# Low halves of 112 weight slots: adding transfers from GpSimd in place of VectorE subtractions, with the negated high half written by ScalarE

## The chip, the core and the metric

The kernel runs on one core of one Trainium2 chip. The core has a matrix engine (TensorE, PE in the profile; its weight loads are the row PEld), VectorE (DVE), ScalarE (ACT), GpSimd (POOL), and SyncE (SP), which here only issues transfers. Sixteen DMA engines move data between the device's memory and the core's on-chip memory. Each compute engine takes its instructions in a fixed order, and an instruction whose input is not ready holds up everything behind it on that engine. The metric is the device time of one execution in microseconds.

## What is computed

Two layers of a decoder on 1024 tokens of width 1024, all in float32. Layer 0 is sliding-window attention (16 query heads, 2 key/value heads, window 128, a learned sink per head, partial rotary), layer 1 a gated linear recurrence (HGRN2, 8 heads). Both have one input projection that also makes a SiLU gate, and an output projection, and each sits between two RMS norms.

```python
def attention_mixer(h, positions, w_in, b_in, sinks, w_out, b_out):
    proj = h @ w_in + b_in
    q, k, v, z = jnp.split(proj, [...], axis=-1)
    ...
    o = sliding_window_gqa(q, k, v, sinks)
    return (o * jax.nn.silu(z)) @ w_out + b_out

def hgrn2_mixer(h, lower_bound, w_in, gnorm_w, w_out):
    proj = h @ w_in
    q, f, i, z = jnp.split(proj, [...], axis=-1)
    ...
    o = chunked_gated_recurrence(q, k, v, log_f)
    o = o * lax.rsqrt(jnp.mean(o * o, axis=-1, keepdims=True) + NORM_EPS) * gnorm_w
    return (o * jax.nn.silu(z)) @ w_out

    for layer in range(DEPTH):
        h = rmsnorm(x, pre_norm_w[layer])
        y = attention_mixer(...) if layer % 2 == 0 else hgrn2_mixer(...)
        x = x + rmsnorm(y, post_norm_w[layer])
```

The four products with weights (`h @ w_in`, `... @ w_out`, twice) are what the change concerns.

## The kernel before

**Split products.** Every product with weights runs as three matmuls of a shorter float type (float32r). Each operand x is split exactly into a high half hi, which is x rounded to that type, and a low half lo = x - hi. `product` (L186 to L189) adds hi*hi, hi*lo and lo*hi into one accumulator. So every weight has to exist twice in on-chip memory, as `whi` and `wlo`.

**The stream of weight slots.** All weights lie in the device's memory as 132 slots of 128 x 512 numbers (256 KB), in the order of use. `fetch` (L131) loads a slot into one of four raw buffers `wraw` by a transfer that SP issues; slot i+4 goes into the buffer of slot i when that is split. `advance` (L137) splits the next slots as far as there are places: ten pairs of `whi` and `wlo` (and two of their own for slots 10 and 11, the keys' weights). For slots 0 to 19 GpSimd makes the high half (L152). From slot 20 on, which is 112 slots, ScalarE makes it by a copy that rounds (L154). The low half is then made by a subtraction, raw - hi (L155), on VectorE, except for slots 2 and 3, which GpSimd subtracts.

**How slots are used and freed.** `used` (L158) counts reads; a slot has eight, and behind the eighth its place is given to the next slot. The projections come in two kinds:

- feature-major (`proj_feat`, L191): a unit makes 128 columns for 512 tokens; two slots hold these columns for all 1024 rows, each is read four times, and a second unit for the other 512 tokens reads them again. Slots 0 to 35 (layer 0's input), 60 to 75 and 84 to 99 (queries and forget gates of layer 1) are of this kind.
- token-major (`proj_nat`, L200): a unit makes 512 columns for 128 tokens; eight slots make a chunk, and each of the chunk's eight units reads all eight slots once, in their order. Slots 36 to 43 and 44 to 51 (layer 0's output, two chunks), 52 to 59 and 76 to 83 (values of layer 1), 100 to 107 and 108 to 115 (its gate), 116 to 123 and 124 to 131 (its output).

A unit has eight steps, one for each 128 rows, and a step is the three matmuls of `product`. In the token-major kind the order is act_hi x whi, act_hi x wlo, act_lo x whi.

**What sets the order.** A planner orders the instructions of each engine by a simulated timeline and priorities; the weight splits have a raised priority (`hp`, L118), so that they go before the work that they make room for. Attention units, projection units and the recurrence's heads are emitted in an order written out by hand (`at`, L577 and following, for layer 0; `plan`, L855 and following, for layer 1).

**Other lines that are named below.** L87 is a helper that passes VectorE instructions on in program order, used at the start. L179 and L180 split activations into halves (ScalarE, VectorE) on their way out of a transpose. In layer 0's last part L615 and L616 take the output projection in, L639 and L640 scale it and add x (VectorE, and GpSimd for one half of L640), L224, L214 and L216 form the reciprocal root mean square `rstd` (ScalarE, GpSimd), L229 normalises (`hn`), and L236 transposes. L473 forms the attention's gates (`th`), L553 masks the probabilities (`pT`). L839 transposes the recurrence's gated output, L846 to L848 gate it, L885, L886 and L888 take the last output projection in.

Of the kernel before, what the change touches and what calls it, by code (L numbers as in the profile page):

```python
# [2 lines left out]
"""Two-layer hybrid decoder trunk (sliding-window attention, then HGRN2) on one core.  # L3

Dense products run as three single-pass float32r products of exactly split operands
(x = hi + lo with 12 significant bits each; hi*hi + hi*lo + lo*hi), which keeps float32's
accuracy.  The other products are plain float32.
"""
# [4 lines left out]
F32 = mybir.dt.float32  # L13
# [19 lines left out]
# rotary frequencies 500000 ** (-j / 8) in float32  # L33
# [17 lines left out]
# columns of the packed constant array  # L51
C_ID, C_INV, C_BIN, C_PRE, C_LB, C_GN, C_SINK = 0, 128, 129, 147, 163, 179, 180
C_N = 196
# columns of the mask array: two for the attention, seven tree levels, causal within blocks of 32
M_L, M_D, M_N = 2 * P, 2 * P + 7 * 64, 3 * P + 7 * 64
# the cheap form of the recurrence's chunks needs every forget gate above this bound
LB_MIN = 2.0 ** -6
LGT_MAX = 4.125  # so that 1 / (1 + exp(LGT_MAX)) > LB_MIN
# [9 lines left out]
# rows of a head in the scores' products: rotated dimensions at 0..8 and 32..40  # L68
# [10 lines left out]
class InOrder:  # L79
    """an engine whose instructions keep the program's order while .on is set"""  # L80
# [9 lines left out]
def emit(tc, I, out):  # L90
# [4 lines left out]
    with top:  # L95
# [22 lines left out]
        def hp():  # L118
            """evictions and weight splits go before the work they make room for"""
            return tc.high_priority(offset=HP)  # L120

        # ---------------- weights: stream of [128, 512] slots, split into hi and lo
# [14 lines left out]
        def advance(end=NS):  # L137
            """fetch and split the next slots, as far as places are free (in program order)"""
            while W["split"] < end:
                i = W["split"]  # L140
                fetch(i + NR)
                if i in (W_K, W_K + 1):
                    W["place"][i] = W["keys"][i - W_K]
                elif W["free"]:
                    W["place"][i] = W["free"].pop(0)
                else:
                    return
                raw, (hi, lo) = wraw[i % NR], W["place"][i]
                with hp():
                    on_pool = i in (2, 3)  # L150
                    if i < 20:
                        nc.gpsimd.tensor_scalar(hi, raw, 1.0, 1.0, op0=ALU.mult, op1=ALU.mult)  # L152
                    else:
                        nc.scalar.activation(hi, raw, AF.Copy)  # L154
                    W["split_ins"][i] = (nc.gpsimd if on_pool else v).tensor_tensor(lo, raw, hi.bitcast(F32), op=ALU.subtract)  # L155
                W["split"] += 1

        def used(i):  # L158
            """one of the eight reads of slot i has been emitted"""
            W["left"][i] = W["left"].get(i, 8) - 1  # L160
            if W["left"][i] == 0:
                if i not in (W_K, W_K + 1):
                    W["free"].append(W["place"][i])
                advance()

        def weight(first, k, c0, c1):
            """hi and lo of columns c0..c1 of the k-th 128 rows of a chunk"""
            hi, lo = W["place"][first + k]
            return hi[:, c0:c1], lo[:, c0:c1]

        # ---------------- activations (feature-major, hi and lo), [k][half]
        act = {(k, h): (actp.tile([P, 512], F32R, name=f"acth{k}_{h}"), actp.tile([P, 512], F32R, name=f"actl{k}_{h}"))
               for k in range(NK) for h in range(2)}
        # at first x, then the first heads' attention, then layer 1's first value columns
# [16 lines left out]
        def proj_feat(first, half):  # L191
            """feature-major [128 columns, 512 tokens]; two slots hold the 128 columns of all k"""
            ps = mm()
            for k in range(NK):
                c = (k % 4) * P
                product(ps, k, weight(first, k // 4, c, c + P), act[k, half])
                used(first + k // 4)
            return ps

        def proj_nat(first, t, c0=0, c1=512, tag="mm"):  # L200
            """token-major [128 tokens, columns c0 to c1 of 512]"""
            ps = mm((P, c1 - c0), tag)
            c = slice((t % 4) * P, (t % 4 + 1) * P)
            for k in range(NK):
                hi, lo = act[k, t // 4]
                product(ps, k, (hi[:, c], lo[:, c]), weight(first, k, c0, c1))
                if c1 == 512:
                    used(first + k)
            return ps

        def rstd_of(pool, ms, width, eps=EPS):
            """(ms + eps) ** -0.5 on [128, width]"""
            m = pool.tile([P, width], F32, tag="ms", bufs=4, name="ms")
            nc.gpsimd.tensor_scalar(m, ms, eps, 1.0, op0=ALU.add, op1=ALU.mult)  # L214
            r = pool.tile([P, width], F32, tag="rstd", bufs=4, name="rstd")
            W["rstd"] = nc.gpsimd.tensor_tensor(r, m, nhalf[:, :width], op=ALU.pow)  # L216
            return r

        def row_rstd(pool, xt, junk=None):
            """of the rows of xt (SBUF [128, 1024])"""  # L220
            if junk is None:
                junk = pool.tile([P, D], F32, tag="jkx", name="jkx")
            ms = pool.tile([P, 1], F32, tag="ss", bufs=4, name="ss")
            nc.scalar.activation(junk, xt, AF.Square, scale=D ** -0.5, accum_out=ms)  # L224
            return rstd_of(pool, ms, 1)

        def norm_rows(pool, xt, hn, r=None):
            """rows of xt over their root mean square"""
# [12 lines left out]
        # =====================================================================  # L241
        # layer 0
# [6 lines left out]
        def halves(t):  # L249
            """columns by which the t-th rows of x are taken; the first half's last rows go in two steps"""  # L250
            return [slice(0, 512), slice(512, D)] if t == 3 else [slice(0, D)]
# [7 lines left out]
        def lower_bounds(sp):  # L259
            """layer 1's lower bounds: softmax over the two rows of logits"""  # L260
# [11 lines left out]
        def rope_tables(sp, cosT, sinT, cosK, tK):  # L272
            """rotary tables; the steps to the angles on [(j, chunk), 64], in turns, and what follows them"""
# [6 lines left out]
            def neg_frac(x):  # L280
                """x = round(x) - x, in two steps"""
# [42 lines left out]
        # =====================================================================  # L324
        # layer 0
        def layer0():
            """attention mixer up to its gated output; leaves x + mixer in x1d and its norm in act"""
# [8 lines left out]
            # of 128 keys from 64 before each block, and the last 64 keys twice  # L336
# [126 lines left out]
            with pool("att", "right") as ap:  # L463
                def z_unit(p, half):
                    ps = proj_feat(20 + 2 * (p ^ 4), half)
                    with hp():
# [4 lines left out]
                        # the last heads' last gates come before their attention, the others after  # L471
# [9 lines left out]
                def values_twice(g, b):  # L481
                    """for the blocks b and b + 1, twice: the former block's earlier 64 keys and the block's later ones"""
# [9 lines left out]
                def attn(g, b):  # L492
# [6 lines left out]
                    for par in range(2):  # L499
                        o = par * 64  # L500
                        # scores of the 128 keys a query may see (their slots: see host_arrays), and 8 x the sink
# [7 lines left out]
                        for hp in range(2):  # L509
# [8 lines left out]
                            # the slots of the block's later half and of the former block's earlier half  # L518
# [21 lines left out]
                        # what lies outside of the 128 keys from 64 before the block, hi and lo below each other  # L540
# [35 lines left out]
                # how many of them to emit behind each attention unit  # L576
# [70 lines left out]
        # =====================================================================  # L647
        # layer 1
        def mixer1(fast, vo, rp):
# [34 lines left out]
            def scores_tree(X, F, Y):  # L684
                """scores[s, t] of all chunks for any gates: products over a binary tree, none above 1.
                Turns X and Y into the queries from the chunk's start and the keys to its end."""
# [43 lines left out]
            def scores_block(h, Q, F, K):  # L730
                """as scores_tree, for gates above LB_MIN: inside blocks of 32 the decay from s to t is a
                quotient of running products from the block's middle, each within LB_MIN ** -16."""
                sc = scs[h % 2]
                # running products of blocks of 16: U up to and with a token, V behind it
# [134 lines left out]
        def output1(fp, last_half):  # L869
# [5 lines left out]
            def unit(c, t):  # L875
                y = fp.tile([P, 512], F32, tag=f"y{c}", bufs=(8, 2)[c], name="y")
                jk = fp.tile([P, 512], F32, tag="jk", name="jk")
                # the last unit in two steps, so that less is left to do at the end
# [41 lines left out]
        # which way the recurrence goes: its lower bounds are 1 / (1 + exp(difference of the logits))  # L920
# [33 lines left out]
def host_arrays(x, positions, pre_norm_w, post_norm_w, attn_w_in, attn_b_in, attn_sinks, attn_w_out, attn_b_out,  # L954
                rec_w_in, rec_lb_logits, rec_gnorm_w, rec_w_out):
    def slots(w):
        """[1024, n * 512] -> [n * 8, 128, 512]"""
# [3 lines left out]
    def slots_feat(w):  # L961
        """[1024, n * 128] -> [n * 2, 128, 4 * 128]: 128 columns of four 128-row blocks to a slot"""
# [27 lines left out]
    # of a query i and a slot j of its merged keys, which begin 64 before a block and wrap around:  # L990
    # where the slot holds the block's later half or the former block's earlier half (first block: any key it may see)
# [31 lines left out]
```

## Time and profile before

| what | value |
|---|---|
| median of three runs | 932.16 us |
| lowest and highest of them | 931.67 and 932.84 us |
| span of the profiled execution, first to last instruction | 930.7 us |
| granted TensorE clock, mean | 0.991 |
| weight slot loads, issued by SP | 132 of 256 KB |
| transfers issued by GpSimd | none |
| DMA engines busy, all queues | 27.5% + 0.4% of 16 engines' span |

The page gives the profiled execution's span and no other time of its own; the median of the unprofiled runs lies 1.5 us above that span. Times in the views are counted from the first instruction of the profiled execution. A row of the groups gives line, engine, operation, what is written and read, shapes and count, then busy time and mean duration, then the idle time of the engine just before, with what ended most of it. A row of the waits names who waited, for whom, the total in microseconds, how often, and the longest. A row of the timeline gives start and length, then engine, line, operation and tiles, and how many instructions it merges.

```profile
wraw<-in_w SPq DMA_DIRECT2D x132, 256.0 KB
```

This is the first row of the list of transfers on the page: what is written and read, who issues, how many, and the size of each.

### The profile page before, as it was taken

The page shows a single profiled execution, that of the slowest core. Times are in us where ns is not written, and L with a number is a line of the kernel's source. Part 1 is how long each engine was busy: PE and PEld are TensorE (multiplying, and loading weights), DVE is VectorE, ACT ScalarE, POOL GpSimd, SP SyncE. Part 2 cuts the span into 40 slices and gives each one's busy share as a digit, 9 for nine tenths or more (in the row PEclk, how much of TensorE's full clock was granted, in tenths as well). Part 3 has the DMA queues.
Part 4 walks back from the last instruction along what each step waited for, and adds up shares of the span by engine and source line. Part 5 has one row for each costly group of instructions (what it writes and reads, how often), then busy time and mean ns, then how long its engine had stood idle before and what let it go on. Part 6 is the DMA issues. An engine that isn't in the chain of part 4 may idle for free.

```text
span 930.7 us, 13298 instructions
## 1 busy us (share of the span) xinstructions
PE 902.9 (97%) x4830; PEld 755.8 (81%) x4830; DVE 551.1 (59%) x895; ACT 373.6 (40%) x958; POOL 355.7 (38%) x514
## 2 busy tenths in 40 slices
PE   6989999999999999989999999999999999999996
PEld 5768888888877788768888888888888888888885
DVE  6859888777776436771266855237765835252233
ACT  6425667666666232542332331333233224142210
POOL 6503455667787105450034532114433633220011
PEclk9998999999999999999999999999999999999998
DMA  8455364512311233440311010121111002022053
GB/s 282 141 151 152 107 184 131 162 55 74 86 44 61 86 91 137 137 147 5 110 56 35 24 46 1 38 72 29 45 46 47 1 1 79 12 81 102 24 181 118
DMA packets 53252, 78.56 MB, mean 84 GB/s; under 512 B 4760, under 2 KB 24984, under 8 KB 53176
## 3 DMA queue, kind: packets, MB, share of 16 engines
q1 hardware_dynamic: 53032, 77.51, 27.5%
q8 instruction: 40, 0.66, 0.3%
q14 instruction: 36, 0.29, 0.1%
q10 hardware_dynamic: 144, 0.10, 0.0%
HBM read 58.89 MB, written 16.88 MB: 81 GB/s over the span
## 4 chain that ended last, share of the span: by engine, by line
PE 55%; DVE 3%; POOL 1%; issue 1%; ACT 1%; DMA 1%; ACTq 0%; POOLq 0%
PE psmm L189 46%; PE pso L825 2%; PE pss L769 2%; PE pso L827 1%; PE psk L812 1%; DVE xn L640 1%; PE pss L790 1%; POOL rstd L216 1%; PE pst L839 1%; PE pst L806 1%; ACT jkx L224 1%; DVE xn L639 1%; PE pss L775 1%; DMA wraw<-in_w 1%; DVE actl L180 0%
## 5 line engine op out<-in xcount | busy, mean ns | idle before, releaser
L189 PE MATMUL psmm<-acth,whi 128*128 128x512 f32 x528 | 209.8, 397 | 1.9 <-DVE th L473 1.0
L189 PE MATMUL psmm<-acth,wlo 128*128 128x512 f32 x528 | 208.8, 395 | 0.2 <-POOL wlo L155 0.2
L189 PE MATMUL psmm<-actl,whi 128*128 128x512 f32 x528 | 208.7, 395 | 0.0
L189 PE MATMUL psmm<-whi,acth 128*128 128x512 f32 (+1 forms) x520 | 202.9, 391 | 0.5 <-DVE th L473 0.4
L189 PE MATMUL psmm<-wlo,acth 128*128 128x512 f32 (+1 forms) x520 | 201.9, 389 | 0.2 <-DVE wlo L155 0.2
L189 PE MATMUL psmm<-whi,actl 128*128 128x512 f32 (+1 forms) x520 | 201.6, 389 | 0.0
L155 DVE TENSOR_TENSOR wlo<-wraw,whi 128x512 fp32r<-128x512 f32 x126 | 92.8, 748 | 114.5 <-ACT whi L154 109.6
L189 PEld LDWEIGHTS psmm<-acth,whi 128*128 128x128 f32 x528 | 99.7, 189 | 22.1 <-DVE th L473 2.1
L189 PEld LDWEIGHTS psmm<-acth,wlo 128*128 128x128 f32 x528 | 99.8, 189 | 19.8 <-POOL wlo L155 0.6
L189 PEld LDWEIGHTS psmm<-whi,acth 128*128 128x128 f32 x520 | 98.0, 189 | 20.6 <-DVE th L473 0.9
L189 PEld LDWEIGHTS psmm<-actl,whi 128*128 128x128 f32 x528 | 99.8, 189 | 18.3
L189 PEld LDWEIGHTS psmm<-whi,actl 128*128 128x128 f32 x520 | 98.0, 188 | 20.5 <-DVE actl L592 0.8
L189 PEld LDWEIGHTS psmm<-wlo,acth 128*128 128x128 f32 x520 | 98.1, 189 | 19.9 <-DVE wlo L155 0.6
L154 ACT ACTIVATE whi<-wraw 128x512 fp32r<-128x512 f32 x112 | 70.2, 630 | 86.6 <-PE psmm L189 66.1
L528 ACT ACTIVATE sm<-sm,st 128x129 f32<-128x129 f32 x128 | 50.0, 393 | 51.9 <-DVE st L526 51.9
L681 POOL TENSOR_SCALAR gate<-gate,lbt 128x512 f32<-128x512 f32 x16 | 15.4, 960 | 131.9 <-ACT gate L679 131.9
L886 DVE TENSOR_TENSOR y<-psmm,wpost 128x512 f32<-128x512 f32 (+1 forms) x17 | 11.2, 659 | 52.4 <-ACT jk L885 49.4
L545 POOL TENSOR_SCALAR_AFFINE_SELECT mY<-pT 64x256 fp32r<-64x256 f32 x56 | 29.2, 522 | 31.7 <-ACT pT L537 26.7
L216 POOL TENSOR_TENSOR rstd<-ms,nhalf 128x1 f32<-128x1 f32 (+1 forms) x48 | 38.8, 809 | 3.4
L785 POOL TENSOR_TENSOR kk<-kk,tt 128x512 f32<-128x512 f32 x16 | 24.9, 1556 | 34.6 <-PE pss L775 28.6
L513 PE MATMUL pss<-KH,QS 128*128 128x256 f32 (+1 forms) x128 | 33.4, 288 | 3.5 <-DMA QS<-qd 3.5
L885 ACT ACTIVATE jk<-psmm 128x512 f32<-128x512 f32 (+1 forms) x17 | 9.7, 571 | 65.6 <-PE psmm L189 65.6
(226 smaller groups left out, 1478.2 us busy)
## 6 DMA issues: line engine op xcount, KB each, us to landing
wraw<-in_w SPq DMA_DIRECT2D x132, 256.0 KB
QS<-qd SPq DMA_DIRECT2D x16, 512.0 KB
xr<-in_x SPq DMA_DIRECT2D x8, 512.0 KB
x1d<-xn SPq DMA_DIRECT2D x8, 512.0 KB
xr<-x1d SPq DMA_DIRECT2D x8, 512.0 KB
out_dram<-xn SPq DMA_DIRECT2D x16, 256.0 KB
xh<-in_x SPq DMA_DIRECT2D x4, 512.0 KB
qd<-qh SPq DMA_DIRECT2D x8, 256.0 KB
```

Source lines behind the costliest of these rows:

```text
L154: nc.scalar.activation(hi, raw, AF.Copy)
L155: W["split_ins"][i] = (nc.gpsimd if on_pool else v).tensor_tensor(lo, raw, hi.bitcast(F32), op=ALU.subtract)
L189: nc.tensor.matmul(ps, a, b, start=(k == 0 and i == 0), stop=(k == NK - 1 and i == 2))
L216: W["rstd"] = nc.gpsimd.tensor_tensor(r, m, nhalf[:, :width], op=ALU.pow)
L513: nc.tensor.matmul(ps[:, i, :nkk], q, KH[:, g, k0:k0 + nkk], start=True, stop=False)
L528: nc.scalar.activation(sm[:, h, :], sm[:, h, :], AF.Exp, bias=nm[:, h:h + 1], scale=0.125, accum_out=dn[:, h:h + 1])
L545: nc.gpsimd.affine_select(mY[r, :, :64], src[64:, :, :64].bitcast(F32), [[0, 4], [-1, 64]], ALU.is_gt, 0.0, base=0, channel_multiplier=1)
L681: nc.gpsimd.tensor_scalar(dst, dst, ol, lb, op0=ALU.mult, op1=ALU.add)
L769: nc.tensor.matmul(ps[:, i, :], V[:, cs], U[:, cs], start=True, stop=True)
L785: nc.gpsimd.tensor_tensor(Yv[:, :, 0, :], Yv[:, :, 0, :], tv[:, :, 1:2].to_broadcast([P, nb, n]), op=ALU.mult)
L825: nc.tensor.matmul(po[:, i, :], sc[:, c, :], vt[:, c, hc], start=True, stop=(c == 0))
L886: v.tensor_tensor(y[:, c0:c1], ps, wpost[:, c * 512 + c0:c * 512 + c1], op=ALU.mult)
```

## The change

For slots 20 to 131 the low half is no longer subtracted. ScalarE writes -hi, the rounded and negated copy of the raw slot, into the place of the low half, then hi as before. GpSimd then issues a transfer that reads the same slot from the device's memory a second time and adds it to what lies there: -hi + raw = lo. Slots 0 to 19 are split as before, with the subtraction moved into their branch. Apart from this, only comments and docstrings are taken out.

```diff
@@ advance
                     if i < 20:
                         nc.gpsimd.tensor_scalar(hi, raw, 1.0, 1.0, op0=ALU.mult, op1=ALU.mult)
+                        W["split_ins"][i] = (nc.gpsimd if on_pool else v).tensor_tensor(lo, raw, hi.bitcast(F32), op=ALU.subtract)
                     else:
+                        nc.scalar.activation(lo, raw, AF.Copy, scale=-1.0)
                         nc.scalar.activation(hi, raw, AF.Copy)
-                    W["split_ins"][i] = (nc.gpsimd if on_pool else v).tensor_tensor(lo, raw, hi.bitcast(F32), op=ALU.subtract)
+                        W["split_ins"][i] = nc.gpsimd.dma_start(lo, I["w"][i], accum_op=ALU.add)
```

## The prediction

> **What bounds the kernel now.** I read the page's first part, then the list of what TensorE (PE) waited for from 95 us on, where the changed slots begin.
>
> ```profile
> span 930.7 us, 13298 instructions
> ## 1 busy us (share of the span) xinstructions
> PE 902.9 (97%) x4830; PEld 755.8 (81%) x4830; DVE 551.1 (59%) x895; ACT 373.6 (40%) x958; POOL 355.7 (38%) x514
> ```
> ```profile
> PE pst L236 <- DVE hn L229: 2.9, 3, 2.4
> PE psmm L189 <- DVE th L473: 1.5, 3, 0.8
> PE pso L556 <- POOL pT L553: 1.4, 4, 0.6
> PE pst L236 <- DVE actl L180: 0.6, 1, 0.6
> PE psmm L189 <- DVE wlo L155: 0.2, 1, 0.2
> ```
> PE is the bound: 902.9 of 930.7 us. Behind 95 us it waits 6.6 us in all (2.9 + 1.5 + 1.4 + 0.6 + 0.2), 5.2 of them on VectorE (DVE), and 0.2 on a low half. So DVE's subtractions, though many, are hidden, and the largest gain that taking work off DVE can bring is about 5 us. What the change can lose is set by how long before its first use a low half is ready.
>
> ```profile
> L155 DVE TENSOR_TENSOR wlo<-wraw,whi 128x512 fp32r<-128x512 f32 x126 | 92.8, 748 | 114.5 <-ACT whi L154 109.6
> ...
> L154 ACT ACTIVATE whi<-wraw 128x512 fp32r<-128x512 f32 x112 | 70.2, 630 | 86.6 <-PE psmm L189 66.1
> ```
> In these groups the numbers behind the count are busy us and mean ns, then idle time before. The high-half copies wait for PE to release a place (66.1 us), and the subtractions for those copies (109.6): both run just in time. Where is just in time close? A slot has eight reads. In the token-major products (slots 36 to 59, 76 to 83, 100 to 131) all eight slots of a chunk are read once per unit, so the last unit of a chunk frees its eight places one by one, and the next unit wants the new slots in the same order; only two of ten places are spare. Take slots 126 to 131 (counted from the loads, which run in order), around 873 us: ScalarE (ACT), the load queue (SP), PE, and the last two subtractions.
>
> ```profile
> 873.89 2.67 ACT L154 ACTIVATE whi<-wraw 128x512 fp32r<-128x512 f32 x4
> 878.15 0.63 ACT L154 ACTIVATE whi<-wraw 128x512 fp32r<-128x512 f32 x1 [1.59 <-DMA wraw<-in_w]
> 880.01 0.63 ACT L154 ACTIVATE whi<-wraw 128x512 fp32r<-128x512 f32 x1 [1.23 <-DMA wraw<-in_w]
> 880.55 0.58 ACT L885 ACTIVATE jk<-psmm 128x512 f32<-128x512 f32 x1
> 881.02 0.19 ACT L885 ACTIVATION_READ_ACCUMULATOR jk<-psmm 128x1 f32 x1
> ```
> ```profile
> 875.31 0.98 SPq L134 DMA_DIRECT2D wraw<-in_w  x2
> ```
> ```profile
> 873.46 0.39 PE L189 MATMUL psmm<-whi,actl 128*128 128x512 f32 x1
> ...
> 878.45 0.39 PE L189 MATMUL psmm<-whi,acth 128*128 128x512 f32 x1
> ...
> 883.43 0.39 PE L189 MATMUL psmm<-wlo,acth 128*128 128x512 f32 x1
> ```
> ```profile
> 878.81 0.69 DVE L155 TENSOR_TENSOR wlo<-wraw,whi 128x512 fp32r<-128x512 f32 x1 [1.53 <-ACT whi L154]
> 880.67 0.69 DVE L155 TENSOR_TENSOR wlo<-wraw,whi 128x512 fp32r<-128x512 f32 x1 [1.17 <-ACT whi L154]
> ```
> The first place is free at 873.85 (873.46 + 0.39). PE starts the next chunk at 878.45 and reads the low half of its eighth slot, 131, at 883.43; seven steps and one matmul lie between, so a step is (883.43 - 878.45 - 0.23) / 7 = 0.68 us, with 0.23 us (a third of it) for one matmul. Slot 131's low half is done at 881.36, 2.07 us early; slot 130's at 879.50, 3.25 us before its use at 882.75.
>
> **The change, part by part.** Removed: 112 subtractions on DVE, 112 x 0.748 = 84 us of DVE, hidden but for some of the 5.2 us above. I credit 1 us, since the longest wait (2.4 us on hn) ends a chain of several engines. Added on ACT: 112 copies, as the row of the same shape 0.63 us each, 70.6 us; ACT goes from 40% to 48% and is nowhere full. But each slot now takes two copies, 1.26 us, where PE frees a place every 0.68. Added on GpSimd (POOL): 112 transfers of 256 KB, each waiting for the negated copy. Added traffic: the raw load stays, as ACT reads it twice, so the weights of these slots are read from memory twice.
>
> At 873.85 ACT now makes twelve copies for slots 126 to 131 (negated, plain, six times): the eleventh ends at 873.89 + 11 x 0.63 = 880.8, and that starts slot 131's transfer. It must be usable by 883.43, so it has 2.6 us; if the square of the unit just ended (0.58 + 0.19 us, quoted) goes ahead on ACT, 1.85. Slot 130's ninth copy ends at 879.55 and leaves 3.2; slot 129's leaves 3.8. So the lag from a negated copy's end to a usable low half decides, and its threshold is 1.85 to 2.6 us.
>
> No transfer is issued from POOL in this trace, and none adds. Its lag in three terms. The transfer itself: the two raw loads issued from 875.31 on, same size, were first used at 878.15 and 880.01; the first took 2.84 us, the second (issued some 0.65 later) 4.05. I take the middle, 3.4. Its issue by POOL:
>
> ```profile
> L134 SPq DMA_DIRECT2D wraw<-in_w x132: 327/328/1515, 4.1 to 876.0; - x132
> ...
> L155 POOL TENSOR_TENSOR wlo<-wraw,whi x2: 1293/1516/1740, 15.2 to 16.4; 128x512 fp32r<-128x512 f32 x2
> ```
> (minimum, median, maximum ns.) Between SP's 0.33, which the 2.84 holds already, and POOL's own 1.74 us for an operation on such a tile: 0 to 1.7 more; I take 0.7. Reading the destination and adding: between nothing and a whole second transfer, 2.8; I take 0.5. Lag: 3.4 + 0.7 + 0.5 = 4.6 us, with ends of 2.8 and 4.05 + 1.7 + 2.8 = 8.6. So PE stalls 4.6 - 2.6 = 2.0 to 4.6 - 1.85 = 2.75 us at such a change of chunk, once; then all its slots are in. I take 2.4. Three changes are of this kind, with no other PE work between the chunks worth a microsecond: to slots 44, 108 and 124. That is 7.2 us.
>
> [...]
>
> Two more changes of chunk have cover.
>
> ```profile
> 831.37 1.91 PE L839 MATMUL pst<-cst,o 128*128 128x128 f32 x16
> ```
> ```profile
> 834.23 1.26 ACT L179 ACTIVATE acth<-pst,cst 128x512 fp32r<-128x512 f32 x2
> ...
> 835.89 1.27 ACT L179 ACTIVATE acth<-pst,cst 128x512 fp32r<-128x512 f32 x2
> ```
> Before slot 116, 1.9 us of transposes come in between, but ACT has their evictions too: I charge 1.5 us. Before slot 52 lies layer 0's last normalisation, where the subtractions do stand in the way:
>
> ```profile
> 398.24 1.32 DVE L155 TENSOR_TENSOR wlo<-wraw,whi 128x512 fp32r<-128x512 f32 x1 [0.38 <-ACT whi L154]
> 399.48 0.68 DVE L640 TENSOR_TENSOR xn<-xn,xr 128x512 f32<-128x512 f32 x1
> ```
> ```profile
> 397.28 1.73 POOL L640 TENSOR_TENSOR xn<-xn,xr 128x512 f32<-128x512 f32 x1 [1.30 <-DVE xn L639]
> ```
> The addition at 399.48 would come up to 1.3 us sooner; but POOL, which adds the other half and makes rstd for the same chain, now issues six transfers among these, and ACT six more copies. I charge 2 us (bounds -1.3 and +6).
>
> What queues behind POOL's new waits? Around 873 us nothing that PE needs soon; in the recurrence (438 to 720 us) gates, keys and rstd.
>
> ```profile
> 403.00:438.00 35.00, 32.58 (x147) 26.85 (x146) 12.40 (x13) 8.64 (x15) 8.16 (x12) 0.95 0.14 47
> 438.00:550.00 112.00, 112.00 (x638) 94.38 (x637) 67.57 (x100) 37.62 (x77) 34.87 (x37) 1.00 0.20 55
> ```
> ```profile
> POOL whi L152 <- PE psmm L189: 34.0, 6, 17.6
> ```
> (First and length of a stretch, then busy PE, PEld, DVE, ACT, POOL, clock, DMA share, GB/s; below: POOL already stood behind PE's release of a place, once 17.6 us long.) From 438 on POOL is 31% busy and PE never idle, and the feature-major units want only two slots each: I charge nothing. Without that cover, a blocked POOL delays gates and rstd by up to such a wait. The load queue gains: a raw buffer is free after ACT's second copy, not after DVE.
>
> Sum: -1 + 7.2 + 1.5 + 2 = +9.7 us on the span of 930.7, which gives 940.4. The median of the three runs, 932.16, lies 1.5 us above that span, and I add that: **942 us**.
>
> **The rivals.** First, *the transfer engines become the bound*: 950 to 975 us, say 962. The transfers from 781 to 789 us, in 40 slices of 0.2 us (busy tenths of the 16 engines, and rate):
>
> ```profile
> DMA  0000000099259930734399999996955977970023
> GB/s 0 0 0 0 0 0 0 0 82 72 41 225 399 348 144 0 51 31 61 133 410 399 379 399 420 379 205 236 297 123 195 287 225 287 410 297 21 0 41 113
> ```
> At a change of chunk the engines already reach 99% and 400 to 420 GB/s with raw loads alone. With adding transfers they are offered 512 KB per 1.26 us, 416 GB/s: just full if adding costs what copying does, and behind by half a microsecond and more per slot if it costs more. That is the point from which it decides. At the upper lag of 8.6 us the three close places cost 6.4 each, the two others some 5.5 each, 30 us in all. [...]
>
> Second, the other side: *faster through the relief of DVE*, 929.5 us. Place: the chain around 384 to 410 us and the attention's gates (th). If the lag is under 2.6 us, nothing stalls, and half of the 5.2 us of waits for DVE go. Against it: the shortest load took 2.84 us, and behind 403 us, where the longest hn wait falls, DVE was busy for only 12.4 of 35 us (row above).
>
> Third, *hidden, and nothing gained*: the lag stays near 2.8, PE loses a few tenths per change, and gains as much: 932 us.
>
> **How the numbers follow.** Forecast 0.45 (own range 936 to 950), full transfer engines 0.25, relief 0.16, hidden 0.14. A measurement of this kernel tells about 0.2% (1.9 us) from no change: the relief counts as faster, hidden as same, the other two as slower: 0.16, 0.14, 0.70. The range of 929 to 963 us leaves out some 0.06 below (most of the relief's 5 us) and 0.12 above.
>
> **What would show it.** PE waits for the low half's transfer at slots 44, 108, 124 of about 2.4 us each, smaller ones near 400 and 835, none in the recurrence; the idle time of DVE grows by some 84 us; memory reads rise by 29 MB (112 x 0.262) from this row:
>
> ```profile
> HBM read 58.89 MB, written 16.88 MB: 81 GB/s over the span
> ```
> The lag from the negated copy's end to PE's restart is 4.6 us. It would be wrong if POOL's issue takes over 1.3 us a transfer, if the scheduler puts copies of later slots ahead of needed ones, or if a waiting POOL holds up the recurrence.

## The result, and the profile after

| | before | after |
|---|---|---|
| median | 932.5 us (4 runs, 931.67 to 933.26) | 961.0 us (4 runs, 959.43 to 963.51) |
| ratio | 1 | 1.0303, 95% interval 1.0281 to 1.0325 |
| span of the profiled execution | 930.7 us | 957.7 us |

The change costs 28.5 us where 9.7 were forecast. Here is the page of the kernel after; in the rows of queues stand packets, MB and their share of sixteen engines' span:

```profile
span 957.7 us, 13479 instructions
## 1 busy us (share of the span) xinstructions
PE 911.3 (95%) x4830; PEld 757.9 (79%) x4830; DVE 483.8 (51%) x783; ACT 430.3 (45%) x1070; POOL 441.0 (46%) x626
...
q1 hardware_dynamic: 53032, 77.51, 25.8%
q0 software_dynamic: 16128, 29.37, 18.5%
...
HBM read 88.25 MB, written 16.88 MB: 110 GB/s over the span
...
L157 POOL DMA_DIRECT2D wlo<-in_w x112 | 100.5, 913 | 159.3 <-ACT wlo L155 110.5
...
L156 ACT ACTIVATE whi<-wraw 128x512 fp32r<-128x512 f32 x112 | 70.1, 626 | 48.6 <-PE psmm L191 41.4
L155 ACT ACTIVATE wlo<-wraw 128x512 fp32r<-128x512 f32 x112 | 69.7, 622 | 26.9 <-DMA wraw<-in_w 19.6
```
Two things grew on PE: its idle time, from 930.7 - 902.9 = 27.8 us to 957.7 - 911.3 = 46.4, and its busy time, by 8.4 us for the same 4830 matmuls. Together these are the 27.0 us of span. Here is the idle time by what PE waited for (total us, times, longest), in the kernel after:

```profile
PE psmm L191 <- DMA wlo<-in_w: 15.5, 17, 2.9
PE psl L930 <- DVE ld L928: 5.5, 1, 5.5
PE pss L515 <- DMA QS<-qd: 3.5, 1, 3.5
PE pso L827 <- DVE S L820: 3.3, 4, 1.0
PE pst L238 <- DVE o L87: 3.2, 2, 2.5
PE pso L561 <- DMA tw<-VX: 2.9, 1, 2.9
```
The first line is the wait that was forecast, on the low half's transfer, seventeen times. The fourth (the state S of the recurrence) and the last (a copy within the chip, in the attention) are new as well and were not forecast. About half of the growth in busy time is the granted clock: its mean is 0.987 where it was 0.991, which is 12.4 us of lost clock in 957.7 against 8.4 in 930.7. The rest probably belongs to the restarts, since a matmul behind a wait takes 0.50 us below where the others take 0.39; that was not taken apart. The clock is 0.83 over the stretch below, around the change to slot 124 (columns as in the stretches of the prediction).

```profile
895.00:915.00 20.00, 17.40 (x62) 12.70 (x61) 1.09 (x2) 6.91 (x15) 5.45 (x7) 0.83 0.57 106
```
Here is PE at that change. A row gives the start, the us of the instruction, and in brackets the idle time before it.

```profile
903.31 0.50 PE L191 MATMUL psmm<-wlo,acth 128*128 128x512 f32 x1 [1.72 <-DMA wlo<-in_w]
903.65 0.40 PE L191 MATMUL psmm<-whi,actl 128*128 128x512 f32 x1
903.88 0.39 PE L191 MATMUL psmm<-whi,acth 128*128 128x512 f32 x1
904.60 0.50 PE L191 MATMUL psmm<-wlo,acth 128*128 128x512 f32 x1 [0.33 <-DMA wlo<-in_w]
...
905.88 0.80 PE L191 MATMUL psmm<-wlo,acth 128*128 128x512 f32 x1 [0.31 <-DMA wlo<-in_w]
906.48 0.63 PE L191 MATMUL psmm<-whi,actl 128*128 128x512 f32 x1
906.90 0.63 PE L191 MATMUL psmm<-whi,acth 128*128 128x512 f32 x1
907.77 0.79 PE L191 MATMUL psmm<-wlo,acth 128*128 128x512 f32 x1 [0.24 <-DMA wlo<-in_w]
...
911.78 0.62 PE L191 MATMUL psmm<-whi,acth 128*128 128x512 f32 x1
912.20 0.43 PE L191 MATMUL psmm<-wlo,acth 128*128 128x512 f32 x1
```
The times at which transfers land, here and below, are taken from the trace's records of landings; PE restarts some 0.04 us behind them (903.31 behind 903.27). PE waits for slot 127, then for 128, 129 and 130: 1.72 + 0.33 + 0.31 + 0.24 = 2.6 us. From about 905.9 to 912.2 its matmuls start 0.42 us apart (906.48, 906.90) instead of 0.23: half the clock. What the place costs is read better from slot 131. PE is 20.7 us behind the kernel before when it comes to this chunk, so the low half that was read at 883.43 before is due at 904.1. Its transfer lands at 909.48, 5.4 us late, and however PE spends that time, waiting or at half the clock, it can't be earlier. The half clock lasts 2.7 us longer than that and loses another 1.3. That is 6.7 us in all; laid beside the trace of before, unit by unit, PE loses 6.5 us here.

The other places, by the same comparison: the change to slot 44 costs 2.6 us, slot 52 about 0.5, slot 108 5.9, slot 116 4.3. With slot 124 that is 19.8 us; the recurrence between them adds 6.3, and the attention and what lies before it about 1.5, less some tenths won back. The 0.5 at slot 52 is a balance and no sign that the place is harmless. PE waits there for the low halves of slots 54, 55 and 59 (stretch from 370 to 460 us):

```profile
PE psmm L191 <- DMA wlo<-in_w: 3.5, 3, 2.9
```
For 3.4 us behind the first of these waits the clock is also halved, by the trace's clock record. In return the 2.4 us that PE waited for hn before, and 3.4 us at half clock just behind that wait (412.4 to 415.9 us of the kernel before), are gone, probably because PE comes later to that chain.

Back at the change to slot 124, these are GpSimd's issues:

```profile
895.60 1.91 POOL L157 DMA_DIRECT2D wlo<-in_w  x2 [0.66 <-ACT wlo L155]
897.67 0.87 POOL L157 DMA_DIRECT2D wlo<-in_w  x1 [0.17 <-issue]
900.28 0.88 POOL L157 DMA_DIRECT2D wlo<-in_w  x1 [1.74 <-ACT whi L156]
903.58 0.88 POOL L157 DMA_DIRECT2D wlo<-in_w  x1 [2.42 <-ACT jk L887]
904.86 0.87 POOL L157 DMA_DIRECT2D wlo<-in_w  x1 [0.41 <-issue]
```
Slot 126's transfer lands at 899.97, 4.8 us after the end of its negated copy: the lag that was forecast as 4.6. But slots 127 to 131 land at 903.27, 904.56, 905.84, 907.73 and 909.48, 7.0 to 8.3 us after theirs. The fourth transfer is issued 0.31 us after the first has landed, the fifth and the sixth 0.31 and 0.30 after the second and the third, although their copies had been ready for 2 to 4 us: three were in flight at most. The names in the brackets (whi, jk) are mere neighbours in time. These are the transfer engines in the same stretch, 894 to 908 us in 40 slices:

```profile
DMA  0000000265999999999999999999931395999696
GB/s 0 0 0 0 0 0 0 47 129 140 334 240 199 205 205 328 263 217 181 158 158 181 211 205 193 199 199 234 176 64 29 35 76 82 170 205 187 88 111 94
```
The engines are full, at some 200 GB/s in most slices, half of the 400 to 420 that full engines moved with raw loads alone before. So there were two suspects for the close places, the engines' own time for an adding transfer and the limit of three in flight, and beside them ScalarE's second copy, the second read of the memory, and GpSimd's waits.

### The profile page after: what moved, and what is told of

Its sections match the earlier page's. It is cut to its first block, busy times and chain, and to the rows that moved or that the text cites. A ratio compares the mean times of both kernels' runs of the same rounds, so it can differ in the third digit from the quotient of the medians.

```text
span 957.7 us, 13479 instructions
## 1 busy us (share of the span) xinstructions
PE 911.3 (95%) x4830; PEld 757.9 (79%) x4830; DVE 483.8 (51%) x783; ACT 430.3 (45%) x1070; POOL 441.0 (46%) x626
## 3 DMA queue, kind: packets, MB, share of 16 engines
q0 software_dynamic: 16128, 29.37, 18.5%
HBM read 88.25 MB, written 16.88 MB: 110 GB/s over the span
## 5 line engine op out<-in xcount | busy, mean ns | idle before, releaser
L191 PE MATMUL psmm<-wlo,acth 128*128 128x512 f32 (+1 forms) x520 | 204.6, 395 | 13.3 <-DMA wlo<-in_w 13.3
L157 POOL DMA_DIRECT2D wlo<-in_w x112 | 100.5, 913 | 159.3 <-ACT wlo L155 110.5
L155 ACT ACTIVATE wlo<-wraw 128x512 fp32r<-128x512 f32 x112 | 69.7, 622 | 26.9 <-DMA wraw<-in_w 19.6
L675 DVE TENSOR_TENSOR qf<-psmm,sg 128x512 f32<-128x512 f32 x16 | 11.0, 688 | 71.7 <-ACT sg L674 71.7
L849 DVE TENSOR_TENSOR sg<-psmm,sg 128x512 f32<-128x512 f32 x16 | 11.1, 691 | 60.3 <-ACT sg L848 60.3
L832 ACT ACTIVATE jk<-pso 128x128 f32<-128x128 f32 x64 | 17.7, 277 | 50.9 <-PE pso L829 49.5
```

Of the source, the lines that this page charges most:

```text
L155: nc.scalar.activation(lo, raw, AF.Copy, scale=-1.0)
L157: W["split_ins"][i] = nc.gpsimd.dma_start(lo, I["w"][i], accum_op=ALU.add)
L191: nc.tensor.matmul(ps, a, b, start=(k == 0 and i == 0), stop=(k == NK - 1 and i == 2))
L675: v.tensor_tensor(dst, ps, sg, op=ALU.mult)
L832: nc.scalar.activation(jk, po[:, i, :], AF.Square, scale=P ** -0.5, accum_out=ss[:, b4 * 4 + i:b4 * 4 + i + 1])
L849: v.tensor_tensor(sg, ps, sg, op=ALU.mult)
```

## The experiments

Each kernel differs from the changed one by the lines shown. Ratios are to the kernel before, timed on the same chip, with their 95% intervals in brackets.

### Room for more transfers in flight

```diff
-    nc = bacc.Bacc("TRN2", ..., dynamic_dma_scratch_size=1024)
+    nc = bacc.Bacc("TRN2", ..., dynamic_dma_scratch_size=2048)
-                        st = ap.tile([P, 3, 4], F32, tag="st", bufs=4, name="st")
+                        st = ap.tile([P, 3, 4], F32, tag="st", bufs=3, name="st")
```

> The changed kernel with 2048 instead of 1024 bytes per partition for the descriptors of GpSimd's transfers (and three instead of four small statistics buffers in the attention, to make room). In the changed kernel GpSimd starts the fourth adding transfer of a burst only 0.3 us after the first has landed. Theory T (the 16 engines are the bound: an adding transfer of 256 KB occupies all of them for 1.58 us, from 176 ns per packet): more transfers in flight help little, at most 1.5 us per change of chunk, 956 to 961 us, and the landings of a burst stay 1.3 us or more apart. Rival R1 (the limit of three in flight sets the pace): the last landing of a burst comes 3 us sooner, 945 to 950 us.

Measured: 956.06 us (954.13 to 957.66), ratio 1.0251 [1.0214, 1.0288]. GpSimd now issues one transfer as soon as ScalarE has made the next negated copy; these are its issues in this kernel's last burst:

```profile
894.88 1.90 POOL L157 DMA_DIRECT2D wlo<-in_w  x2 [0.62 <-ACT wlo L155]
896.95 0.87 POOL L157 DMA_DIRECT2D wlo<-in_w  x1 [0.17 <-issue]
897.99 0.87 POOL L157 DMA_DIRECT2D wlo<-in_w  x1 [0.18 <-issue]
899.03 0.87 POOL L157 DMA_DIRECT2D wlo<-in_w  x1 [0.17 <-issue]
```
and PE still waits, once per slot:

```profile
901.90 0.50 PE L191 MATMUL psmm<-wlo,acth 128*128 128x512 f32 x1 [0.99 <-DMA wlo<-in_w]
...
903.18 0.50 PE L191 MATMUL psmm<-wlo,acth 128*128 128x512 f32 x1 [0.32 <-DMA wlo<-in_w]
...
904.48 0.49 PE L191 MATMUL psmm<-wlo,acth 128*128 128x512 f32 x1 [0.34 <-DMA wlo<-in_w]
...
905.76 0.50 PE L191 MATMUL psmm<-wlo,acth 128*128 128x512 f32 x1 [0.32 <-DMA wlo<-in_w]
```
The restarts are 1.28 to 1.30 us apart: with nothing holding them back, adding transfers of 256 KB land every 1.29 us here, while PE reads a new low half every 0.68. The 1.58 us of the expectation was too long: it puts the packets' times one behind the other on each of sixteen engines, and they overlap in part. In the kernel after, from 900 to 904 us, they come to 1.06 of sixteen engines' time. The limit of three is worth about 5 of the 28 us (961.0 - 956.1; the two ratios differ by 0.5%, and their intervals just overlap); the larger part remains without it. The smaller statistics buffer, which made room, was not timed by itself.

### The close slots alone, and the others alone

The low halves of 30 slots are first read right after a change of chunk in the token-major products; the other 82 have time.

```diff
+        CLOSE = [j for a in (46, 54, 110, 118, 126) for j in range(a, a + 6)]
-                    else:
+                    elif i in CLOSE:        # acc_not_close: elif i not in CLOSE
                         nc.scalar.activation(lo, raw, AF.Copy, scale=-1.0)
                         nc.scalar.activation(hi, raw, AF.Copy)
                         W["split_ins"][i] = nc.gpsimd.dma_start(lo, I["w"][i], accum_op=ALU.add)
+                    else:
+                        nc.scalar.activation(hi, raw, AF.Copy)
+                        W["split_ins"][i] = (nc.gpsimd if on_pool else v).tensor_tensor(lo, raw, hi.bitcast(F32), op=ALU.subtract)
```

> The complement: adding transfers only for the 30 close slots, VectorE for the other 82. Theory T: nearly the whole loss at the changes of chunk, 949 to 954 us. R2 and R3 as the main cause: 30 of 112 slots bring a quarter of 28 us, 939 to 941 us.

> Adding transfers only for the 82 slots that are not wanted at once; the 30 close ones (46-51, 54-59, 110-115, 118-123, 126-131) are subtracted on VectorE as before. Theory T: the loss at the changes of chunk goes (about 19 of 28 us), 939 to 944 us remain for attention and recurrence. Rivals R2 (ScalarE's second copy) and R3 (GpSimd's queue held up by its new waits), if they were the main cause: the loss is spread over all slots and 950 us or more remain.

Measured: the close slots alone 950.48 us (946.28 to 952.83), ratio 1.0183 [1.0138, 1.0228]; the others alone 941.22 us (939.01 to 944.83), ratio 1.010 [1.0058, 1.0143]. Against 931.82 for the kernel before that is +18.7 and +9.4, in sum 28.1 against 28.5 for the whole: the two parts add up, within the 4 us or so to which each is known, and two thirds of the loss hang on 30 slots. With these alone PE waits on the low halves 14.1 us in 12 waits, nearly as long as with all. But the 82 slots that have time cost 9 us, and that needed another look.

### Copies in place of additions

The transfers copy the slot over the negated half instead of adding it, so the low halves hold the whole weights; issues, waits, queue, order and the second read of the memory stay.

```diff
-                        W["split_ins"][i] = nc.gpsimd.dma_start(lo, I["w"][i], accum_op=ALU.add)
+                        W["split_ins"][i] = nc.gpsimd.dma_start(lo, I["w"][i])
```

> The changed kernel with the addition left out: GpSimd's transfers copy the raw slot into the place of the low half instead of adding to it, so the low halves hold the whole weights. Issue, waits, bytes from memory and ScalarE's copies stay. Theory T: what costs is the engine time of adding (1.58 us for 256 KB against some 0.65 of a copy), so most of the loss at the changes of chunk goes: 938 to 945 us, landings of a burst about 1 us apart. If reading memory twice or the issue from GpSimd were the cause, adding or not: 955 us or more.

Measured: 932.46 us (930.84 to 933.98), ratio 1.0002 [0.9983, 1.002], below the 938 to 945 that were expected. These rows are from this kernel's page and from its list of PE's waits:

```profile
q0 software_dynamic: 16128, 29.37, 10.7%
```
```profile
PE psmm L191 <- DMA wlo<-in_w: 2.7, 4, 2.0
PE pso L827 <- DVE S L820: 2.5, 4, 0.8
```
The same 16128 packets with the same bytes took 18.5% of 957.7 us when they added and take 10.7% of 931.1 when they copy: 0.185 x 16 x 957.7 / 16128 = 176 ns against 0.107 x 16 x 931.1 / 16128 = 99 ns a packet, on the average over the queue's packets. (A transfer is 144 of them, 128 of 2 KB and 16 of 4 bytes; in the changed kernel's trace the 2 KB packets alone take 178 ns in the median.) The difference shows in the burst of slots 127 to 130. With copies the landings are 0.57 to 0.66 us apart, and the lag falls from 5.5 to 4.2 us; with additions they are 1.28 to 1.89 apart, and it rises from 7.0 to 8.3. With copies nothing is lost in the sum: by the trace PE is about 5 us ahead at the end of the attention, loses 3.8 in the recurrence and the rest at the changes of chunk. So neither ScalarE's second copies nor GpSimd's waits nor the doubled reads cost the 28 us as such. What costs them is the addition, above all the transfer engines' time for it, and besides that the limit of three in flight, which copies did not meet (up to five were in flight), and GpSimd's longer issue. The four waits on S stay, and come up again below.

### Adding from a tile on the chip

```diff
-                        W["split_ins"][i] = nc.gpsimd.dma_start(lo, I["w"][i], accum_op=ALU.add)
+                        W["split_ins"][i] = nc.gpsimd.dma_start(lo, raw, accum_op=ALU.add)
```

> The transfer adds from the raw buffer on the chip instead of reading the slot from memory again; the raw buffer is freed only when that has landed. Theory T: an adding transfer takes the engines as long, 955 to 970 us (raw loads start later). If the second read of memory were the cost, its bursts would shorten and the time fall to 945 us or less.

Measured: 963.29 us (956.26 to 965.78), ratio 1.0303 [1.0252, 1.0354], as slow as the change itself, though it reads no slot twice from the memory. Its page shows the same share for the same packets, and the reads of the kernel before:

```profile
q0 software_dynamic: 16128, 29.37, 18.5%
...
HBM read 58.89 MB, written 16.88 MB: 79 GB/s over the span
```
With the addend read from a tile on the chip a packet takes 0.185 x 16 x 964.0 / 16128 = 177 ns, with the addend from the memory 176, as a copy 99: here it made no difference where the addend came from; that the transfers add did. The kernels' times agree less cleanly than they look: the transfers land sooner here (4.2 us behind the start of the issue in the median, where the changed kernel has 5.1), but they hold the raw buffers until they have landed, so that the next loads start later (ScalarE's negated copies wait 34.9 us for raw loads, where the changed kernel has 19.6).

### The slots with time: attention and recurrence

The edit is that of the close slots, with `elif i < 46` (attention, as slots below 20 are in the branch ahead) or `elif 60 <= i < 110` (recurrence) as condition.

> Adding transfers only for slots 20 to 45 (attention and layer 0's first output chunk), VectorE for the others. The changed kernel lost 2.1 us up to the first token-major unit: 932 to 936 us if that is the transfers' doing; 931 or less if it is not.

> Adding transfers only for slots 60 to 109 (recurrence and its neighbours), VectorE for the others. In the changed kernel these stretches grew by 6.3 us, where the prediction charged nothing. If the transfers or GpSimd's waits for them hold up the recurrence: 936 to 940 us. If the growth came only from the different start after earlier stalls: 930 to 934 us.

Measured: attention alone 936.11 us (932.93 to 938.91), ratio 1.0035 [1.0015, 1.0055], at the upper end of what was expected; recurrence alone 937.1 us (934.31 to 939.34), ratio 1.0049 [1.0031, 1.0066]. With the close slots this makes 3.9 + 4.9 + 18.7 = 27.5 of the 28.5 us. In the attention PE's list shows two waits on transfers:

```profile
PE pso L564 <- DMA tw<-VX: 3.2, 1, 3.2
PE psmm L194 <- DMA wlo<-in_w: 2.6, 3, 1.3
```
The first is a copy of 32 to 64 KB within the chip, issued by SP. In the kernel before PE doesn't wait for it, with copies in place of the additions 0.9 us, with additions 2.1 to 4.9 us in the five kernels that have them in the attention. That it is late because it shares the engines with adding packets is the likely reading; it wasn't tried alone. In the recurrence PE waits on no transfer; the loss shows on DVE (kernel with adding in the recurrence alone):

```profile
518.25 2.28 DVE L744 TENSOR_TENSOR_SCAN U<-gate,F 128x1024 f32<-128x1024 f32 x1
520.45 2.26 DVE L745 TENSOR_TENSOR_SCAN V<-gate,E 128x1024 f32<-128x1024 f32 x1
522.63 0.32 DVE L823 SCALAR_TENSOR_TENSOR S<-S,tt,psk 128x128 f32<-128x128 f32 x1
```
```profile
523.00 0.49 PE L830 MATMUL pso<-o,sc 128*128 128x128 f32 x2 [1.03 <-DVE S L823]
```
The last update of S, which PE needs, stands on DVE behind two scans of the next head, 4.4 us of work. Before the change all updates of a head came ahead of them at this place. An update of S stands directly behind two scans in four places of this kernel, and nowhere in the kernel before or in the one with the close slots alone, which has no wait on S either. It does so in four places of the kernel with copies too, where PE also waits for S four times. The planner orders by a simulated timeline, in which DVE, without the subtractions, is free earlier. To part this from the transfers, DVE's subtractions were put back beside them: the kernel with adding in the recurrence alone, and one line more.

### VectorE's subtractions kept beside the adding transfers

```diff
                         W["split_ins"][i] = nc.gpsimd.dma_start(lo, I["w"][i], accum_op=ALU.add)
+                        v.tensor_tensor(raw, raw, hi.bitcast(F32), op=ALU.subtract)
```

> As acc_rec (adding transfers for slots 60 to 109 alone, 937.1 us against 932.2), with VectorE's 50 subtractions kept beside them: VectorE subtracts in place, in the raw tile, after ScalarE's two copies, and nobody reads what it writes. VectorE's load in the recurrence is again that of before, and so, nearly, is the order in which the planner puts its instructions: in 2 places, where acc_rec has it for nearly every early head, a last update of S still stands behind the two scans. Theory A (most of the 5 us are the planner's new order on VectorE, where updates of S come behind two scans of 2.3 us each): TensorE's waits for S fall from 3.3 us to 1.7 or less, and the time to 933 to 935. Theory B (the adding transfers themselves disturb the recurrence, by raw tiles that come free later and SP's loads that are slower beside them): the waits on S may go but the time stays at 936 to 938. If VectorE's relief was worth something in the recurrence, the time rises above 938.

Measured: 933.87 us (931.86 to 936.34) beside 932.79 for the kernel before, ratio 1.001 [0.9995, 1.0024]. The two rows are the recurrence of the kernel with adding alone, and of the one with DVE's work kept:

```profile
460.00:790.00 330.00, 326.10 (x2012) 276.66 (x2011) 162.44 (x242) 120.48 (x311) 149.63 (x156) 1.00 0.32 66
```
```profile
460.00:790.00 330.00, 329.96 (x2038) 280.37 (x2036) 196.56 (x286) 122.91 (x315) 151.78 (x158) 1.00 0.34 69
```
DVE has 34 us more work in this stretch and PE is idle for 0.04 us instead of 3.9; the waits on S are gone, in the two places too where an update still stands behind the scans. The transfers are the same in both. So in the recurrence it is the work taken from DVE that costs time, and the transfers cost what is left, about 1 us (up to 2.2 by the interval). That it costs by the order in which the rest is then put is the likely reading and not wholly shown, since two of the four places keep that order without a wait. Which estimate in the planner tips the order wasn't tried.

### ScalarE's second copy without transfers

Both copies on ScalarE, and DVE adds the raw slot to the negated half, so that DVE has as much to do as before.

```diff
-                        W["split_ins"][i] = nc.gpsimd.dma_start(lo, I["w"][i], accum_op=ALU.add)
+                        W["split_ins"][i] = v.tensor_tensor(lo, raw, lo.bitcast(F32), op=ALU.add)
```

> ScalarE's two copies as in the changed kernel, but VectorE adds the raw slot to the negated half in place of the transfer; nothing is issued from GpSimd. Theory T: the copies are hidden, 931 to 937 us. Rival R2 (ScalarE's second copy makes the slots late, 1.04 instead of 0.62 us per slot): 945 us or more.

Measured: 929.08 us (926.73 to 931.62) beside 931.82, ratio 0.9979 [0.9958, 0.9999], below the 931 to 937 that were expected. The second copy costs nothing. The kernel even looked a little faster than the one before, so it was timed again:

> The same kernel as act_neg_dve_add (ScalarE writes both copies, VectorE adds the raw half to the negated one, no adding transfer), which took 929.08 us against 932.17, ratio 0.9979 with an interval that ends at 0.9996 of one. If the gain is real: 928 to 930 us again, ratio 0.996 to 0.9985, with TensorE's window at half clock near 67 us shorter than before's 6.8 us and hardly a wait near 410 us. If it was the scatter of that batch: within 0.1% of before.

Measured: 931.1 us (928.72 to 932.33) beside 932.79, ratio 0.998 [0.9967, 0.9993]. The ratio repeats, 0.2% or 2 us, and no other version was timed below the kernel before. (The batch above gave 931.82 and 0.9999 where the expectation has 932.17 and 0.9996.) Where the 2 us come from stays open. The window at half clock near 67 us was expected to be shorter; in the first profile it was, in the second the clock over the first 95 us is 0.96 as in the kernel before, and the longest wait for hn is 2.7 us against 2.4. In that profile the gain lies in the attention (up to 5 us ahead at 270 us, of which 1.6 last). The adding costs DVE what the subtracting did (747 ns each on the average, against 748), so it is no relief of DVE.

## Why the prediction was wrong in its size, point by point

**The bound and the places: right.** PE was the bound, low halves were ready just in time, and most of the loss sits at the changes of chunk that were named: slots 44, 108, 124 and 116. With adding on the 30 slots there and at slot 52, and nowhere else, 18.7 of the 28.5 us remain.

**The step that failed is "Reading the destination and adding ... I take 0.5".** It put the whole price of the addition into the lag of one transfer, and then took that lag, 4.6 us, for the transfer that PE needs last, as if each ran on empty engines. For the first of a burst it holds: 4.8 us measured. But a packet takes 176 ns with the addition and 99 without, the engines deliver an added slot only every 1.29 us, PE wants one every 0.68, and ScalarE starts one every 1.04. The queue grows from slot to slot, the other five of the six land 7.0 to 8.3 us after their copies, near the upper end of 8.6, and PE does not stall "once" with all slots in behind it, but once per slot. The term was a rate and was entered as a delay. This is the first rival, *the transfer engines become the bound*, with the point from which it decides (adding costs more than copying) and nearly its time, 962 us. The copies in place of additions, at 932.5 us, are that rival's counter-test.

**Sizes.** The forecast had 2.4 us each for slots 44, 108 and 124, 1.5 for 116 and 2 for 52; found were 2.6, 5.9, 6.5, 4.3 and 0.5. Slot 44 agrees by luck: the lags of its burst are 4.9 to 9.3 us, but PE had other units' matmuls to run: between the waits for slots 47 and 50, which end at 346.89 and 353.50 us, it is never idle, though slots 48 and 49 land only at 349.07 and 351.38. Slot 52 is the balance shown above, a stall with half clock against a wait and a half clock saved. At slot 124 the excess is mostly in the lag: slot 131's is 7.8 us where 4.6 were taken, 3.2 more, and the due time, 2.4 us after its copy's end, lies within the threshold of 1.85 to 2.6 that was forecast. The forecast had no term for the clock, which falls to half behind these stalls and adds 1.3 here. Slot 116's transposes, charged as partial cover, covered little.

**GpSimd's issue, 0.7 us: right enough.** It takes 0.88 in the bursts (mean 0.913), below the 1.3 named as the point where it would matter. What the forecast did not see is that GpSimd also holds the fourth transfer back until the first has landed (0.31 us behind that landing, as shown above). By the kernel with 2048 bytes that costs about 5 us.

**The recurrence, "I charge nothing": wrong, by 5 us.** The reason given (POOL is free, two slots a unit are few) stands: PE waits on no low half there. The loss came from the side that the forecast took for a gain, less work on DVE, probably through the planner's order. So the relief of DVE, credited with 1 us and the ground of the second rival, has the other sign in the recurrence. In the attention it is not shown to gain: between 95 and 300 us PE gets ahead by 4 us in the kernel with copies, but by 3 in the kernel that leaves DVE its work and only has ScalarE's second copies.

**The attention, for which the sum has no term: 4 us.** PE waits there for SP's copies (tw) and for three low halves. With copies in place of the additions it gains instead, so this too is the addition's price.

**What the forecast said would show.** Memory reads rise by 29 MB: 88.25 - 58.89 = 29.4. ScalarE's copies take 0.62 us each and cost nothing, as charged. DVE's idle time grew by 94 us, 27 of them the longer span; its busy time fell by 67 rather than 84 us.

**The third rival, a lag near 2.8 us: not met.** From the start of the issue to the landing, the shortest copy here took 2.8 us and the median one 4.0; with the addition they took 3.8 and 5.1. The load from SP that the 2.84 us was read from is matched by the shortest copy alone; additions and a full queue took longer.

**One set of engines for both queues.** The first rival takes it that transfers from GpSimd and from SP load the same sixteen engines. The runs agree: from 798 to 812 us of the kernel after, GpSimd's queue takes 72.1% of sixteen engines' time and SP's 26.4%, and the engines are 99% busy in all; and PE waited 2.1 to 4.9 us for SP's copies (tw) in the five kernels with adding transfers in the attention.

## What to carry to other kernels

Moving an operation into a transfer buys engine time with transfer time: ask first at what rate the engines deliver such transfers in a burst, not only how late one of them comes, and compare it with the rate at which the bound engine consumes them (here one every 1.29 us against one every 0.68). Replacing the adding transfer by a copying one tells in one run whether the addition or everything around it costs. And taking work off an engine that isn't the bound can cost time, as it did in the recurrence here (3.9 us of waiting for PE, 0.04 with the work put back), probably because the planner reorders what is left; putting the work back beside the new path parts the two.

## What the runs showed of the hardware that was not expected

- A packet of GpSimd's transfers took 176 ns on the average with the addition and 99 as a copy, and 177 with an addend read from a tile on the chip and not from the device's memory (from 18.5%, 10.7% and 18.5% of sixteen engines' time for 16128 packets). In a burst adding transfers of 256 KB landed 1.29 us apart where 2048 bytes were set aside, and 1.28 to 1.89 where 1024 were; copies 0.57 to 0.66.
- With 1024 bytes set aside for GpSimd's transfers three adding ones of 128 x 2 KB were in flight at most; with 2048 five were issued without a pause. With copies and 1024 bytes up to five were in flight, without such a pause.
- GpSimd's issue of an adding transfer takes 0.88 us, that of a copying one 0.54 (medians over 112).
- Behind short stalls in a row PE ran at half the clock, by its matmuls, 0.42 us apart against 0.23, for 6.3 us; the trace's clock record has 0.50 for 6.83 us, from 905.43 to 912.25. In the kernel with 2048 bytes, whose four stalls at the same place come to 2.0 us instead of 2.6, it did not (granted clock 1.00 from 893 to 910 us). In the clock records of the kernels before and after there are seven halved stretches ahead of the last 20 us; five last 3.41 us and two 6.83. In the 3.41 us just ahead of each, PE was idle for 1.62 to 2.95 us, the least ahead of the fall shown here (902.02 to 905.43 us). But from 857.64 to 861.05 us of the kernel after it was idle for 1.70 us, and the full clock stayed. So the idle time alone did not decide; what else does, no run here shows.
